# A mixer layer on one core: bank accesses in the planner's reckoning, one last block of 512 columns, and three column blocks at the start

## The chip, the cores and the metric

One of the eight cores of a Trainium2 chip runs the kernel. The metric is the device time of one execution in microseconds (us). A core has TensorE (PE, matrix products; PEld is its weight loading), VectorE (DVE), ScalarE (ACT), GpSimd (POOL) and SyncE (SP), each with an instruction stream of its own; they wait for one another by semaphores. SBUF is the on-chip memory that operands come from, PSUM the one that products are summed in, here eight banks of 128 x 512 numbers.

## The reference

One layer of a streaming encoder: 512 tokens of 2,048 numbers are projected, mixed along time by two groups of heads, projected back, added to the input and normalised.

```python
proj = einsum('btd,dc->btc', h, w_in)              # 2048 -> 8320 columns
rw = token_shift(proj[..., :RWKV_COLS], shift_mu)  # first 4224 columns
hg = proj[..., RWKV_COLS:]
o_rwkv = rwkv7_branch(rw, ...)   # 16 heads of 64: r, k, v, z and two low-rank parts
o_hgrn = hgrn2_branch(hg, ...)   # 8 heads of 128: q, f, i, z (g in the kernel)
y = einsum('btc,cd->btd', concatenate([o_rwkv, o_hgrn], -1), w_out)
h = layer_norm(ALPHA * h + y, ln_w, ln_b)
```

## The kernel before

Everything is in float32. A product of float32 accuracy is made of three of a faster kind: each operand is split into a rounded part (ScalarE copies it, suffix h) and the rest (VectorE subtracts, suffix l), and `three` multiplies h by h, h by l and l by h into one PSUM bank.

The tokens are transposed in 16 tiles of 128 channels x 512 tokens (`xh`, `xl`), which stay in SBUF. The projection goes by blocks of 128 columns (`proj`): 16 tiles x 3 products of 512 columns each. Weights come from `w_all` in loads of 512 KB into two raw buffers (`wr`); each holds two quarters, and a quarter is split into `wh` and `wl`, of which there are three each (`ready`, `part`). A raw buffer is loaded again when both its quarters are split.

At the start two column blocks, w0 (the low-rank columns) and k0, are multiplied together token tile by token tile while the tiles arrive. `first` fetches the weight quarters, `token` the tiles, all in SP's queue; the first weight quarter is cut after 128 columns. Nine products with a zero tile (`WARM`) run before.

Between the projection's products stand the mixers': per head pair a preparation, an inversion, a scan of eight chunks, and a finish for RWKV; per HGRN head masked products of chunks. Their small products write PSUM banks tagged `mix` (two) and `acc` (two), the projections the four `main` banks. The gated outputs of all heads (`gated`) are spilled and read again for the output projection.

What runs when is decided while the program is built, by `Plan`. It keeps an estimated clock for each engine and queues of threads (generators of operations). `until` and `three` advance TensorE's clock with the large products; `pump` issues the next operation of each thread whose operands are estimated to be ready at about the present time (`step`, `start`, `seen`). A product that a thread offers is issued only if its start, as `start` has it, is not later than TensorE's present time less a lead of 0.35 us; otherwise the next large products go first. The order of instructions on each engine is then fixed; on the chip each waits by semaphores for what it really needs, and that includes the last engine that used its PSUM bank.

The output projection goes by blocks of columns, and within a block by the 16 gated tiles (`rows`): each tile of weights is multiplied with four row blocks of 128 tokens, in four banks. There are three blocks of 512 columns and two of 256; of the last one, the row blocks are done one after another, from weights that are all split by then. For each row block and column block `row_out` adds the input (VectorE reads PSUM), takes statistics (`bn_stats`), and after the last column block `finish` computes mean and variance, GpSimd the power -1/2 of the variance (`rsqrt`), and then each row is normalised. In `finish` the first 512 to 768 columns (`POOL_COLS`) are scaled by ScalarE and multiplied and added to on GpSimd (`early`), the others are done on VectorE (`late`): times the norm's weight beforehand (`premultiply`), less the weighted mean, times the factor plus the norm's bias, two or three passes in all. Outputs leave from SP's queue and ScalarE's.

Of the kernel before, what the change touches and what calls it, by code (L numbers as in the profile page):

```python
# [15 lines left out]
P = 128  # L16
# [36 lines left out]

SETS = {AF.Sigmoid: ("sigmoid",), AF.Tanh: ("exp", "sigmoid"), AF.Exp: ("exp",)}


class Plan:
# [11 lines left out]
    def __init__(self, room):  # L69
        self.clock = {"pe": 0.0, "dve": 0.0, "act": 0.0, "pool": 0.0, "dma": 0.0}  # L70
        self.table = None
        self.narrow = False
        self.queues = []
        self.ready, self.busy = {}, {}
        self.room = room
        self.slots = {tag: [(0, 0.0)] * n for tag, n in room.items()}
        self.count, self.used = 0, {}

    def start(self, e, op):

        t = 0.0
        for r in op.reads:
            t = max(t, self.seen(r, e))
        for w in op.writes:
            x, by = self.busy.get(w, (0.0, e))
            if e != "pe" or by is None:
                t = max(t, x if by == e else x + self.AFTER[by])
        return t

# [117 lines left out]
def mixer_kernel(ctx, tc, x_t, x_r, w_all, par, up, ln_wb, consts, hmask, out):  # L207
# [25 lines left out]
    def take(tag, shape=(P, T), dt=F32):  # L233
# [5 lines left out]
        if tag in PBUFS:  # L239
            t = ppool.tile(list(shape), dt, tag=tag, name=nm(tag), bufs=PBUFS[tag])  # L240
        else:
# [137 lines left out]
    def ready(i, tags=("wh", "wl")):  # L379

        if i < 2 * nload and i not in parts:
            parts[i] = tuple(st(t, [P, QT], F32R) for t in tags)

            def run():
                yield from split(*parts[i], raws[i // 2][:, i % 2 * QT : i % 2 * QT + QT])
                if i % 2:
# [19 lines left out]
    def part(i, width):  # L406
# [3 lines left out]
        plan.until(lambda: by_now(lo))  # L410
# [27 lines left out]
    def rows(q, width, lh, ll, fin, order=range(KT), hook=None, tags=("main",), early=None):  # L438
# [3 lines left out]
        for j in range(KT // per):  # L442
# [3 lines left out]
            for t in range(4):  # L446
                if j == 0:
                    pss.append(main_ps(tags)[:, :width])
                if early:
                    for i in early[j][t - 1 : t]:  # L450
                        ready(q + i, ("t", "t") if i in IN_T else ("wh", "wl"))
                elif 0 < t < 3:
# [605 lines left out]
    u0, u1 = unit(), unit()  # L1058
# [5 lines left out]
    plan.clock["pe"] = T0  # L1064
# [3 lines left out]
    def first(q, tag):  # L1068

        if q >= 4:  # L1070
            raw = take("g")
        elif q % 2 == 0:
# [4 lines left out]
        src = w_all[q // 2, :, q % 2 * QT : q % 2 * QT + QT]  # L1077

        def bring(c0, c1):
            nc.sync.dma_start(raw[:, c0:c1], src[:, c0:c1])  # L1080
            plan.fetched(raw, 4 * (c1 - c0))

            def run():
                if q not in parts:
                    parts[q] = tuple(st(t, [P, QT], F32R) for t in ((tag, tag) if tag else ("wh", "wl")))
                hi, lo = parts[q]
                yield from split(hi[:, c0:c1], lo[:, c0:c1], raw[:, c0:c1])
                if c1 < QT:
                    return
                if q >= 4:  # L1090
                    drop(raw)
                elif q % 2:
                    load(2 * u1 + 2 + q // 2)

            return run

        return bring

    def token(k):
# [8 lines left out]
        return run  # L1108

    plan.clock["dma"] = 0.7  # L1110
    arrive = []

    def fetch(k):
        a = []
        if k % 4 == 0:
            w0, w1 = first(4 * u0 + k // 4, None), first(4 * u1 + k // 4, "q4")
        if k == 0:

            a = [w0(0, P), token(k), w1(0, P), w0(P, QT), w1(P, QT)]
        elif k % 4 == 0:  # L1120
            a = [w0(0, QT), token(k), w1(0, QT)]
        else:
            a = [token(k)]
        arrive.append(a)

    for k in range(12):
        fetch(k)
    ps0, ps1 = main_ps(), main_ps()
    queued = 0
    for k in range(KT):  # L1130
        while queued < min(k + 5, KT):
            for run in arrive[queued]:
                plan.add(splits, run())
            queued += 1
        if 2 <= k < 6:
            plan.until(room(t=1))
# [3 lines left out]
        if k >= 13:  # L1140
            ready(4 * u1 + k - 9)
        qs = (4 * u0 + k // 4, 4 * u1 + k // 4)
        plan.until(lambda: by_now(xl[k]) and all(q in parts and by_now(parts[q][1]) for q in qs))
        for ps, q in zip((ps0, ps1), qs):
            hi, lo = (a.rearrange("p (k c) -> p k c", c=P) for a in parts[q])
            three(ps, hi[:, k % 4], lo[:, k % 4], xh[k], xl[k], k == 0, k == KT - 1)
# [58 lines left out]
    for name, j in _order()[1:]:  # L1205
# [30 lines left out]
        if (name, j) == ("k", 0):  # L1236
            ps = ps1
# [10 lines left out]
    sums, earlies, norms = plan.queue(), plan.queue(), plan.queue()  # L1248
    stats = cpool.tile([P, 4, 5, 6], F32, tag="stats", name="stats")
# [3 lines left out]
    POOL_COLS = (768, 640, 512, 512)  # L1253
    blocks = [(0, 512), (512, 512), (1024, 512), (1536, 256), (1792, 256)]
# [6 lines left out]
    def cuts(c0, c1):  # L1261

        return [(max(c0, d * T), min(c1, d * T + T)) for d in range(4) if max(c0, d * T) < min(c1, d * T + T)]

# [3 lines left out]
    def premultiply(t, c0, c1):  # L1268

        c0 = max(c0, POOL_COLS[t])  # L1270
        if c0 < c1:
            y, w = ys[t][c0 // T][:, c0 % T : (c1 - 1) % T + 1], lnw[0][:, 0, c0:c1]
            k = y_keys(t, c0, c1)
            yield keyed(Op([dve_tt_way(y, y, w), pool_tt_way(y, y, w)], [], []), k, k)

    def finish(t):
        mv, rs = take("mv", [P, 4]), take("rs", [P, 1])
        k_st, k_mv, k_v, k_n, k_r, k_m = ([f"{n}{t}"] for n in ("stat", "mean", "var", "neg", "rstd", "bias"))
        yield keyed(Op([("dve", 0.1, lambda: dve.bn_aggr(mv[:, 0:2], stats[:, t]))], [], []), k_st, k_mv + k_v)
        yield keyed(ts(mv[:, 1:2], mv[:, 1:2], LN_EPS, None, ALU.add), k_v, k_v)  # L1280
        yield keyed(ts(mv[:, 2:3], mv[:, 0:1], -1.0, None, ALU.mult), k_mv, k_n)
# [185 lines left out]
```

## Time and profile before

| | us |
|---|---|
| median of three runs (lowest, highest) | 1121.27 (1120.59, 1122.06) |
| the profiled execution | 1123.09 |
| its span, first to last instruction | 1121.3 |
| TensorE busy in it | 1091.5 |
| VectorE, ScalarE, GpSimd busy | 766.5, 456.3, 88.6 |

A row of a profile gives start and length in us, the engine, the line, the operation with the tile written, an arrow and the tiles read, the size in partitions x elements, and in brackets how long the engine was idle before and what it waited for. "x3" stands for three instructions in a row. TensorE's products are pipelined: their starts follow one another every 0.23 us while each is shown 0.39 us long. The granted clock is the share of TensorE's full clock that the chip lets through; on average it was 0.991.

### The profile page before, as it was taken

Reading aid. Unit: us, or ns where it says so; the run is one execution under the profiler, and the core shown is the slowest. Engines: PE = TensorE matmul, PEld = TensorE weight load, DVE = VectorE, ACT = ScalarE, POOL = GpSimd, SP = SyncE. Lnnn points to the kernel's source line nnn. Section 1 sums busy time; section 2 is a strip of 40 time slices with the busy share of each in tenths; the row PEclk is TensorE's granted clock in tenths of the full one; section 3 lists DMA queues with packets and bytes.
Section 4 is the critical chain, followed back from the end, with each engine's and each line's share of the span. In section 5 each row is a group of like instructions: output and inputs, shape, how many; then the busy total and the mean of one; then the engine's idle time right before and its main releaser. Section 6 shows DMA issues by size and latency. Waiting matters only on the chain.

```text
span 1121.3 us, 19205 instructions
## 1 busy us (share of the span) xinstructions
PE 1091.5 (97%) x7402; PEld 901.8 (80%) x7402; DVE 766.5 (68%) x1739; ACT 456.3 (41%) x1042; POOL 88.6 (8%) x163
## 2 busy tenths in 40 slices
PE   8999999999999999999999999999999999999994
PEld 7878878788888878788887888888887778888893
DVE  6658967645579767857986774657976776624468
ACT  6532365433332465534245552433346444322221
POOL 0000000000010000101000010001000010000015
PEclk8999999999999999999999999999999999999997
DMA  7222211133323311223231122322231145433433
GB/s 274 85 80 93 95 59 58 57 99 94 90 75 103 96 58 59 67 79 117 76 104 58 58 76 87 99 92 77 94 102 46 52 141 194 136 122 110 144 126 138
DMA packets 36667, 108.50 MB, mean 97 GB/s; under 512 B 4320, under 2 KB 6496, under 8 KB 36448
## 3 DMA queue, kind: packets, MB, share of 16 engines
q1 hardware_dynamic: 34848, 104.33, 29.2%
q10 hardware_dynamic: 1728, 2.95, 0.7%
q8 instruction: 58, 0.95, 0.4%
q14 instruction: 33, 0.27, 0.1%
HBM read 99.92 MB, written 7.34 MB: 96 GB/s over the span
## 4 chain that ended last, share of the span: by engine, by line
PE 89%; DVE 6%; ACT 2%; issue 1%; DMA 1%; POOL 0%; SPq 0%; DVEq 0%; ACTq 0%
PE main L396 68%; PE mix L288 10%; PE mix L396 3%; PE acc L396 3%; PE acc L288 3%; PE mix L292 2%; DVE q L320 1%; DVE wl L311 1%; DVE t L311 1%; ACT z L301 1%; DVE bd L320 1%; ACT wh L301 1%; DMA t<-x_t 0%; DVE inv L320 0%; DMA t<-spill 0%
## 5 line engine op out<-in xcount | busy, mean ns | idle before, releaser
L396 PE MATMUL main<-xh,wh 128*128 128x512 f32 x896 | 358.0, 400 | 2.2 <-ACT xh L301 2.2
L396 PE MATMUL main<-xh,wl 128*128 128x512 f32 x896 | 356.6, 398 | 0.0
L396 PE MATMUL main<-xl,wh 128*128 128x512 f32 x896 | 356.0, 397 | 0.0
L301 ACT ACTIVATE wh<-wr 128x512 fp32r<-128x512 f32 (+1 forms) x313 | 195.5, 626 | 268.9 <-PE main L396 203.9
L311 DVE TENSOR_TENSOR wl<-wr,wh 128x512 fp32r<-128x512 f32 (+1 forms) x313 | 213.5, 683 | 130.2 <-ACT wh L301 126.9
L396 PEld LDWEIGHTS main<-xh,wh 128*128 128x128 f32 x896 | 169.1, 189 | 36.0 <-ACT xh L301 2.6
L396 PEld LDWEIGHTS main<-xl,wh 128*128 128x128 f32 x896 | 168.9, 188 | 33.8 <-DVE xl L311 0.8
L396 PEld LDWEIGHTS main<-xh,wl 128*128 128x128 f32 x896 | 168.9, 189 | 33.5
L396 PE MATMUL main<-wh,xh 128*128 128x512 f32 (+1 forms) x272 | 108.0, 397 | 1.9 <-DVE t L320 1.9
L396 PE MATMUL main<-wh,xl 128*128 128x512 f32 (+1 forms) x272 | 108.1, 397 | 0.0
L396 PE MATMUL main<-wl,xh 128*128 128x512 f32 (+1 forms) x272 | 107.4, 395 | 0.0
L301 ACT ACTIVATE z<-mix 64x64 f32<-64x64 f32 (+1 forms) x245 | 56.0, 229 | 92.1 <-DVE bd L320 71.4
L396 PEld LDWEIGHTS main<-wh,xh 128*128 128x128 f32 x272 | 51.3, 189 | 10.4 <-DVE t L320 2.3
L396 PEld LDWEIGHTS main<-wh,xl 128*128 128x128 f32 x272 | 51.3, 189 | 8.6
L396 PEld LDWEIGHTS main<-wl,xh 128*128 128x128 f32 x272 | 51.3, 189 | 8.2
L302 ACT ACTIVATE t<-main,om 128x512 f32<-128x512 f32 x33 | 22.6, 688 | 61.2 <-PE main L396 61.1
L320 DVE SCALAR_TENSOR_TENSOR bd<-mix,pc,bd 64x64 f32<-64x64 f32 x112 | 31.2, 283 | 22.4 <-PE mix L288 17.2
L343 POOL TENSOR_TENSOR rs<-rs,mhalf 128x8 f32<-128x8 f32 (+1 forms) x16 | 25.1, 1572 | 250.3 <-DVE rs L316 129.5
L311 DVE TENSOR_TENSOR inv<-inv 64x30 f32<-64x30 f32 (+14 forms) x120 | 38.6, 322 | 3.1
L311 DVE TENSOR_TENSOR inv<-inv,inv 64x30 f32<-64x30 f32 (+14 forms) x120 | 38.6, 322 | 2.9
L346 POOL MEMSET z<- 64x128 f32 x64 | 11.9, 199 | 355.7 <-PE acc L288 312.1
L311 DVE TENSOR_TENSOR t<-t,tot 128x256 f32<-128x256 f32 x96 | 38.4, 416 | 0.2
(207 smaller groups left out, 1489.1 us busy)
## 6 DMA issues: line engine op xcount, KB each, us to landing
wr<-w_all SPq DMA_DIRECT2D x158, 512.0 KB, 3.5
t<-x_t SPq DMA_DIRECT2D x16, 256.0 KB, 5.6
g<-x_r SPq DMA_DIRECT2D x16, 256.0 KB, 4.2
spill<-g SPq DMA_DIRECT2D x12, 256.0 KB, 4.3
t<-spill SPq DMA_DIRECT2D x12, 256.0 KB, 4.0
big<-ln_wb SPq DMA_DIRECT2D x1, 2048.0 KB, 9.1
out<-q ACTq DMA_DIRECT2D x7, 256.0 KB, 2.4
up<-up SPq DMA_DIRECT2D x8, 128.0 KB, 2.8
```

The lines of the kernel that those rows point to most:

```text
L288: return Op([("pe", cost, lambda: pe.matmul(o, l, r, start=start, stop=stop, **kw))], [l, r], [o], narrow=narrow)
L292: return Op([("pe", 0.11, lambda: pe.transpose(o, i, ident))], [i], [o])
L301: return "act", cost, lambda: sc_e.activation(o, i, f, scale=scale)
L302: return "act", cost, lambda: sc_e.activation(o, i, f, scale=scale, bias=bias)
L311: return dve_op([a, b], o, lambda: dve.tensor_tensor(o, a, b, f), base=0.16 if o.shape[0] < P and size(o) == C and o.tensor.name in tags e ...
L320: return dve_op([a, b], o, lambda: dve.scalar_tensor_tensor(o, a, s, b, f1, f2), per=0.00113, base=0.085 if o.shape[0] == P else 0.25 if s ...
L343: lambda: pool.tensor_tensor(o, i, mhalf[:, : size(o)], ALU.pow))], [i], [o])
L346: return Op([("pool", 0.1, lambda: pool.memset(o, v))], [], [o])
L396: pe.matmul(ps, l, r, start=first and i == 0, stop=last and i == 2)
```

## The change

There are three parts.

The planner. Each PSUM tile's name is kept in `banks`. An operation that reads a bank now counts as ready only after the bank's last use by any engine (`done`), and a product that writes one after the last use by another engine; before, a product that wrote a bank took no account of readers of the same tile.

The start. Three blocks, w0, k0 and r0, are multiplied together. The weight quarters of the first four tiles are cut in three, 128, 128 and 256 columns; the three first pieces are issued from ScalarE's queue, everything else from SP's. Tile 0's nine products go in the order h by h for the three blocks, then l by h, then h by l.

The end. The last 1,024 columns are two blocks of 512. The weights of the last one are fetched along with those of the one before, in alternation (`_last_quarters`), and are kept split in SBUF, in tiles tagged `t`, `ksq` and `ia` that the mixers no longer need and in `wh` and `wl`. Its row blocks follow one another, as those of the last 256 columns did. GpSimd computes only the rsqrt. Of each row block all four pieces of 512 columns are scaled by ScalarE and multiplied and added to by VectorE; in the last row block ScalarE and VectorE share them, the first two (`AHEAD`) going the way of `late`. All outputs leave from SP's queue.

```diff
@@ class Plan
         for r in op.reads:
             t = max(t, self.seen(r, e))
+            if r in self.banks:
+                t = max(t, self.done(r, e))
         for w in op.writes:
-            x, by = self.busy.get(w, (0.0, e))
-            if e != "pe" or by is None:
-                t = max(t, x if by == e else x + self.AFTER[by])
+            t = max(t, self.done(w, e))
         return t
+
+    def done(self, name, e):
+        x, by = self.busy.get(name, (0.0, e))
+        return (0.0 if e == "pe" else x) if by == e else x + self.AFTER[by]
@@ start
-    u0, u1 = unit(), unit()
+    us = [unit() for _ in range(3)]
...
+            ws = [first(a, 0) for a in range(3)]
+            for bring, run in ws:
+                bring(0, P, nc.scalar)
+            x0 = token(0)
+            for bring, run in ws:
+                bring(P, 2 * P)
...
+            fetch(1)
+            for bring, run in ws:
+                bring(2 * P, QT)
...
+        if k == 0:
+            for i, (low, x) in enumerate(((0, xh[0]), (1, xh[0]), (0, xl[0]))):
+                for ps, q in zip(pss, qs):
...
+                    begin_one(ps, parts[q][low][:, :P], x, i)
@@ end
+def _last_quarters():
+    o = [(2, 0)] + [(d, n + 3 - d) for n in range(13) for d in (2, 3)]
+    return o + [(2, 14), (2, 15), (3, 13), (3, 14), (3, 15)]
...
-    POOL_COLS = (768, 640, 512, 512)
-    blocks = [(0, 512), (512, 512), (1024, 512), (1536, 256), (1792, 256)]
...
+        def last(d):
+            y, w, b, o, k = columns(d)
+            if d in first:
+                yield keyed(stt(y, y, rs, b, ALU.mult, ALU.add), k + k_r, k)
+            else:
+                yield keyed(tt(y, y, b, ALU.add), k, k)
+            nc.sync.dma_start(o, y)
...
+        for d in rest:
+            y, w, b, o, k = columns(d)
+            yield keyed(Op([("act", 0.6, lambda y=y: sc_e.activation(
+                y, y, AF.Identity, scale=rs, bias=mv[:, 3:4]))], [], []), k + k_r + k_m, k)
```

At the start, SP's queue (x_t are token tiles, w_all the weights, into wr, g and t for the three blocks), before:

```order
L1080 DMA wr_122<-w_all 128x128
L1101 DMA t_125<-x_t 128x512
L1080 DMA g_123<-w_all 128x128
L1080 DMA wr_122<-w_all 128x384
L1080 DMA g_123<-w_all 128x384
L1101 DMA t_130<-x_t 128x512
```

and now:

```order
L1117 DMA t_128<-x_t 128x512
L1092 DMA wr_122<-w_all 128x128
L1092 DMA g_123<-w_all 128x128
L1092 DMA t_124<-w_all 128x128
L1117 DMA t_133<-x_t 128x512
L1092 DMA wr_122<-w_all 128x256
```

Token tile 0 is now SP's first transfer and tile 1 its fifth, where they were the second and the sixth; the three small pieces for tile 0 have gone to ScalarE's queue, whose beginning is now:

```order
L1092 DMA wr_122<-w_all 128x128
L1092 DMA g_123<-w_all 128x128
L1092 DMA t_124<-w_all 128x128
L313 ACT_TABLE_LOAD
L313 ACTIVATE wh_170<-wr_122 128x128
L313 ACTIVATE xh_68<-t_128 128x512
```

It began with the table load and the same two splits; the three issues stand ahead of them.

In the scans of the mixers' second group, on TensorE (rt, z, bt, bd are tiles of a scan, main<-xh products of the projection), before:

```order
L288 MATMUL acc_4212<-bd_3737,q_2928 128x128
L292 MATMUL mix_4230<-cst,q_2929 128x128
L396 MATMUL main_4123<-xl_90,wh_4086 128x512
L396 MATMUL main_4123<-xh_74,wl_4087 128x512
L288 MATMUL acc_4222<-bd_3718,q_2550 128x128
L292 MATMUL mix_4241<-cst,q_2551 128x128
L292 MATMUL mix_4241<-cst,t_2846 128x128
```

and now:

```order
L300 MATMUL acc_4319<-bd_3730,q_2562 128x128
L411 MATMUL main_4103<-xh_82,wh_4216 128x512
L411 MATMUL main_4103<-xl_98,wh_4216 128x512
L304 MATMUL mix_4378<-cst,q_2563 128x128
L304 MATMUL mix_4378<-cst,t_2858 128x128
L411 MATMUL main_4103<-xh_82,wl_4217 128x512
```

Between a scan's product into acc and the transposes into mix that follow it stand two products of the projection now, where they followed one another; the places differ all along the scans in this way.

At the end, VectorE's work on the last row block, from its evacuation on (g is the input, big the norm's weight and bias, inv the row block, mv and rs its statistics), before:

```order
L320 SCALAR_TENSOR_TENSOR inv_9737<-g_10561,main_10833 128x256
L1336 BN_STATS stats<-inv_9737 128x6
L1279 BN_AGGR mv_10910<-stats 128x2
L316 TENSOR_SCALAR mv_10910<-mv_10910 128x1 x2
L333 TENSOR_TENSOR inv_9737<-inv_9737,big_9548 128x256
L320 SCALAR_TENSOR_TENSOR inv_9736<-big_9548,mv_10910,inv_9736 128x512
L320 SCALAR_TENSOR_TENSOR inv_9737<-big_9548,mv_10910,inv_9737 128x512
L320 SCALAR_TENSOR_TENSOR inv_9736<-inv_9736,rs_10911,big_9548 128x512
L320 SCALAR_TENSOR_TENSOR inv_9737<-big_9548,mv_10910,inv_9737 128x512
L320 SCALAR_TENSOR_TENSOR inv_9737<-inv_9737,rs_10911,big_9548 128x512 x2
```

and now:

```order
L332 SCALAR_TENSOR_TENSOR inv_9749<-g_10645,mix_10623 128x512
L1389 BN_STATS stats<-inv_9749 128x6
L1331 BN_AGGR mv_10700<-stats 128x2
L328 TENSOR_SCALAR mv_10700<-mv_10700 128x1 x2
L332 SCALAR_TENSOR_TENSOR inv_9748<-big_9587,mv_10700,inv_9748 128x512
L332 SCALAR_TENSOR_TENSOR mv_10700<-mv_10700,rs_10701 128x1
L332 SCALAR_TENSOR_TENSOR inv_9748<-big_9587,mv_10700,inv_9748 128x512
L332 SCALAR_TENSOR_TENSOR inv_9748<-inv_9748,rs_10701,big_9587 128x512
L323 TENSOR_TENSOR inv_9749<-inv_9749,big_9587 128x512
L332 SCALAR_TENSOR_TENSOR inv_9748<-inv_9748,rs_10701,big_9587 128x512
L323 TENSOR_TENSOR inv_9749<-inv_9749,big_9587 128x512 x3
```

Evacuation and statistics are 512 wide instead of 256, the multiplication that stood behind them is gone, the bias of the row (mv from rs) has come over from GpSimd, and two pieces take a multiplication and an addition behind ScalarE's scaling.

More of the change, by code (lines that the diff above doesn't have):

```diff
@@ L1384, in mixer_kernel @@
     for t in range(4):
         sl = slice(t * P, t * P + P)
[L1386 removed]
+        ps = main_ps(banks)
         for n, k in enumerate(korder):
[L1388 to L1390 removed]
+            if t == 0 and n == 1:
+                quarters(len(seq))
+            if n == 4:
+                residual(t, 3)
+            hi, lo = part(q0 + seq.index((3, n)), T)
+            three(ps, gh[k][:, sl], gl[k][:, sl], hi, lo, n == 0, n == KT - 1)
```

313 lines of the change are left out of this document (175 added, 138 removed).

## Prediction

> **What bounds the kernel now.** I read the page first, then busy time by stretch, then the timeline of the first 17 us and the last 65 us, then who waited for whom. The page says TensorE:
>
> ```profile
> span 1121.3 us, 19205 instructions
> PE 1091.5 (97%) x7402; PEld 901.8 (80%) x7402; DVE 766.5 (68%) x1739; ACT 456.3 (41%) x1042; POOL 88.6 (8%) x163
> ```
>
> TensorE is idle for 29.8 us of the span. Nothing the change does removes a product, so its gain has to come out of those 29.8 us, out of stretches where TensorE is busy at a worse rate, or out of the work after its last matmul. The next rows (columns: stretch, its length, then busy time of PE, PEld, DVE, ACT, POOL, the granted clock, DMA share, GB/s) say where the idle time in the middle lies.
>
> ```profile
> 25.00:900.00 875.00, 867.43 (x6182) 709.34 (x6180) 620.44 (x1471) 375.96 (x901) 56.85 (x127) 1.00 0.26 81
> 900.00:950.00 50.00, 47.71 (x276) 39.03 (x275) 37.77 (x87) 22.96 (x49) 5.85 (x3) 1.00 0.45 152
> 950.00:1104.00 154.00, 154.00 (x869) 135.54 (x868) 80.66 (x137) 38.68 (x64) 15.56 (x15) 1.00 0.41 136
> ```
>
> 875 us hold 7.57 us of idle TensorE, the 50 us after them 2.29, the last 154 none. So three places matter: the start, the mixers (9.86 us in all), and the end.
>
> **Part 1, the start.**
>
> ```profile
> 0.74 0.38 SPq L1080 DMA_DIRECT2D wr<-w_all  x1
> 3.06 1.38 SPq L1101 DMA_DIRECT2D t<-x_t  x3
> 4.92 0.64 PE L396 MATMUL main<-xh,wh 128*128 128x512 f32 x1
> 6.55 0.39 PE L396 MATMUL main<-xh,q 128*128 128x512 f32 x1
> 8.40 2.01 ACT L301 ACTIVATE xh<-t 128x512 fp32r<-128x512 f32 x3 [0.33 <-DMA t<-x_t]
> 9.09 0.80 PE L396 MATMUL main<-xh,wh 128*128 128x512 f32 x1 [2.15 <-ACT xh L301]
> 8.50:9.00 0.50, 0.00 (x0) 0.00 (x0) 0.16 (x1) 0.50 (x1) 0.00 (x0) 0.68 1.06 410
> 9.09 30.21 PE main L396 x118
> 1014.94 43.52 PE main L396 x192
> ```
>
> The last row is the rate of undisturbed 512-wide products: 43.52 / 192 = 0.2267 us each. TensorE does the six products of token tile 0 from 4.92 to 6.55 and then sits 2.15 us until tile 1, issued at 3.06, has landed at 8.4 and been split. In that gap the granted clock falls: 0.68 in the half microsecond 8.5 to 9.0 means that it fell to half at about 8.7. The chain row has 118 products take 30.21 us from 9.09; at 0.2267 they need 26.75, so the half clock costs 3.46. The start loses 9.09 - 6 x 0.2267 + 3.46 = 11.2 us against a TensorE that were busy from time 0.
>
> With three column blocks tile 0 feeds nine products and tile 1 nine more. Tile 1 is then the transfer that completes 896 KB of arrivals (six weight pieces of 64 KB and two tiles of 256 KB) where it completes 1,024 KB now (64 + 256 + 64 + 192 + 192 + 256), and it is the fifth issue on SP instead of the sixth: at SP's spacing of 0.47 us (0.74 to 3.06 is five issues) it goes out at 2.6. The first three pieces leave from ScalarE's queue, ahead of its table load, so splitting begins later, at about 3.4 instead of 2.7, but tile 0 is what the first product waits for and it leaves 0.43 earlier. Bounds for the start of tile 1's products: 9.09 as now (twice as many small pieces may eat what is saved) and 7.0, where the nine products of tile 0, from about 4.9, end and nothing is waited for. I take 8.3, in the upper half: 0.44 for the issue, and of one eighth of the 5.3 us between its issue and its landing (0.67) half, since small pieces moved slowly. With the nine products done at 7.0 TensorE waits 1.3 us, not 2.15. From there it has 9 x 0.2267 = 2.04 us of work per token tile, more than ScalarE's 2.01 / 3 = 0.67 per tile plus three weight splits every four tiles, so it should not wait again beyond some 0.3 us for the second half of the first weight quarters. If the clock stays whole the start then loses 8.3 - 9 x 0.2267 + 0.3 = 6.6: a gain of 4.6. If it falls again, 3.46 of this is lost: a gain of about 1.2.
>
> Does it fall? The gap of 2.15 us did it. A gap of the same kind later did not:
>
> ```profile
> 920.68 0.50 PE L396 MATMUL main<-wh,xh 128*128 128x512 f32 x1 [1.92 <-DVE t L320]
> ```
>
> Here TensorE was idle 1.92 us and the row of 900 to 950 above keeps a granted clock of 1.00. So 1.3 us should be survived; I give that 0.7. The Trainium skill, "TensorE: Matmul & The Clock Gate", section on the HAM clock gate, says that the clock is halved only after an idle window of about 3.4 us. By that rule neither gap would have halved it, and no gap of 1.3 us would; the row at 8.5 disagrees, so the rule does not raise the chance above what the two rows give.
>
> The other work of the third block is only moved: its 48 products, 4 weight splits on ScalarE and VectorE and 1 MB of loads stood in the first block's successors before. SP gets no wait that was not there; ScalarE's queue holds three issues ahead of its first split.
>
> **Part 2, the last 512 columns and the norm.** Now two blocks of 256 columns:
>
> ```profile
> 1058.46:1081.49 23.03, 23.03 (x194) 23.03 (x194) 14.67 (x26) 8.19 (x14) 1.17 (x1) 1.00 0.55 183
> 1081.49:1104.53 23.04, 23.04 (x193) 22.83 (x191) 21.01 (x43) 2.73 (x4) 11.98 (x13) 1.00 0.24 89
> ```
>
> 384 products of 256 columns take 46.07 us, with weight loading busy all the time; 192 of 512 take 43.52. That is 2.55 us off TensorE with nothing beside it, so off the end.
>
> After TensorE's last matmul (end 1104.53) VectorE is still at work on the third row block:
>
> ```profile
> 1109.81 0.41 DVE L320 SCALAR_TENSOR_TENSOR inv<-g,main 128x256 f32<-128x256 f32 x1
> 1110.71 0.29 DVE L1279 BATCH_NORM_AGGREGATE mv<-stats 128x2 f32<-128x30 f32 x1
> 1111.04 0.21 DVE L316 TENSOR_SCALAR mv<-mv 128x1 f32<-128x1 f32 x2
> 1111.27 0.72 POOL L343 TENSOR_TENSOR rs<-mv,mhalf 128x1 f32<-128x1 f32 x1 [1.93 <-DVE mv L316]
> 1111.50 1.41 DVE L320 SCALAR_TENSOR_TENSOR inv<-big,mv,inv 128x512 f32<-128x512 f32 x2
> 1112.33 0.81 ACT L1294 ACTIVATE inv<-inv,mv,rs 128x512 f32<-128x512 f32 x1 [6.21 <-DMA out<-q]
> 1113.49 1.75 DVE L320 SCALAR_TENSOR_TENSOR inv<-big,mv,inv 128x512 f32<-128x512 f32 x1
> 1115.16 2.41 DVE L320 SCALAR_TENSOR_TENSOR inv<-inv,rs,big 128x512 f32<-128x512 f32 x2
> 1056.03 0.39 PE L396 MATMUL main<-wh,xl 128*128 128x512 f32 x1
> 1056.46 0.69 DVE L320 SCALAR_TENSOR_TENSOR q<-g,main 128x512 f32<-128x512 f32 x1 [2.04 <-PE main L396]
> 1057.18 0.69 DVE L1336 BATCH_NORM_STATS2 stats<-q 128x6 f32<-128x512 f32 x1
> 1068.81 1.29 DVE L311 TENSOR_TENSOR t<-wr,t 128x512 fp32r<-128x512 f32 x2
> ```
>
> The last block's evacuation starts at 1109.81, 5.28 us after TensorE ended. From there the chain is 11.49 us to the end of the span, of which the last 3.73 (1117.57 to 1121.3) are the output's transfer. Next to GpSimd's two 512-wide operations a VectorE operation of 0.74 took 1.75.
>
> In the new block each row block has 48 x 0.2267 = 10.88 us on TensorE. VectorE's chain for one of the first three, by these rows: evacuation 0.72, statistics 0.72, aggregate 0.33, variance 0.13, GpSimd's rsqrt to 1.05 after that, bias and ScalarE's first scaling 1.05 (0.81 and two hand-overs), eight multiplications or additions at 0.61 (1.29 for two) 4.9: 8.9 us. It is done 2 us before the next block arrives, so the backlog of 5.28 goes, and the last evacuation starts 0.43 after the start of the last product (1056.03 to 1056.46). Its own chain from the evacuation on: 0.72 + 0.72 + 0.33 + 0.13, first mean subtraction 0.66 beside the rsqrt, bias at 2.85, second subtraction to 3.6, then two scale-and-add at 0.66 and four multiplications or additions at 0.61, the last to its full 0.69: 7.42. ScalarE's two scalings (2 x 0.81 from 3.05, so to 4.6) are finished before VectorE asks for them at 4.26 and 5.5. With 3.73 for the output 11.15 us, against 11.49: wider evacuation and statistics cost 0.6, GpSimd's absence gives more than that back.
>
> So, in the time of this execution: last product at 1058.30 + 191 x 0.2267 = 1101.6, evacuation at 1102.0, end at 1113.2: 8.1 us earlier, 2.5 of it TensorE's and 5.6 the tail's.
>
> Against it stand the loads. The weights of the last two blocks now all come interleaved, two quarters for each 2.72 us of products (12 x 0.2267) over 13 steps, through two raw buffers.
>
> ```profile
> 1068.14 1.15 ACT L301 ACTIVATE t<-wr 128x512 fp32r<-128x512 f32 x2 [0.38 <-DMA wr<-w_all]
> 1068.91 0.33 SPq L376 DMA_DIRECT2D wr<-w_all  x1
> 1074.92 0.33 SPq L376 DMA_DIRECT2D wr<-w_all  x1
> DMA to landing us min/median/max: 3.4/3.7/5.4
> ```
>
> One buffer's round was 6.0 us there (1068.91 to 1074.92); 3.7 to landing and 2.0 for the two splits (1068.14 to 1070.1) make 5.7. The two buffers must come round every 5.44. Each round loses 0.3 to 0.6, over six and a half rounds 2 to 4 us, against a lead of two steps less the split, about 2.7 at its start. I charge 0.5 us; bounds 0 and 3.4 (6.5 x 0.56, and 0.65 for each of four residual tiles that join the queue, less the lead). End part: 7.6.
>
> **Part 3, the mixers.** The planner now lets an operation on a PSUM bank wait for the bank's last user, as the chip does.
>
> ```profile
> PE acc L288 <- DVE t L311: 2.4, 8, 0.4
> PE mix L288 <- DVE nr L327: 1.7, 2, 0.8
> ```
>
> Such waits, of a small product behind VectorE, are what the 9.86 us of idle consist of. Where the planner expects them, it puts projection products in front: in the order of the program, from the first to the last acc-from-bd product of a group's scans, there are 135, 136, 144 and 147 of them before and 157, 159, 171 and 176 after, with the number of changes between large and small products all but equal (638 and 642). The products themselves are only moved, and TensorE is full beside them, so I cost the moving at nothing; if the scans got longer in time, the cover is the projection, which after the last small product still has 677 products (641 before) to run. Bounds: the whole 9.86 gained, or 3 lost (the 1.92 wait above and one of 0.8 once more). I take 4, less than half: one wait of 1.92 is for the evacuation of a projection, which the rule does not touch, and late operands remain late.
>
> **Sum.** 4.6 + 7.6 + 4.0 = 16.2. The profiled execution took 1123.09 us with a span of 1121.3, so 1106.9 with a span of 1105.1. The median of the runs is 1121.27, 1.8 below that execution: 1105.1.
>
> **Rivals.** (1) The clock falls at the start all the same: 1105.1 + 3.4 = 1108.5. For it: it did, and the gap may be longer than 1.3. (2) The planner's rule moves products and frees nothing, since the late operands are late for other reasons: 1109.1; for it, the 1.92 wait. (3) The last blocks' weights come late as bounded above: 1105.1 + 2.9 = 1108.0; against it, TensorE has no idle time in 950 to 1104 with buffers at the same round. (4) Slower: the scans' chain stretches in time. It has 56 acc-from-bd steps, two heads side by side, so 28 in a row; 16.2 us of gain are gone if each is later by 0.58 us and the output blocks then wait for the last gated tiles. But 36 more products (8.2 us) stand between, so it decides from 24.4 / 28 = 0.87 us a step, and gives 1121.3 + 28 - 24.4 = 1124.9 at 1 us a step. The planner's 22 to 29 more products per group are 5 to 6.6 us for 7 steps, of this size; against it, the small products end earlier in the order, not later.
>
> **Chances.** Forecast 0.42, (1) 0.25, (2) 0.16, (3) 0.1, (4) 0.03; 0.04 for all of the mixers' idle time gained (1099). Two of the middle rivals together give 1112. Range 1100 to 1113. 0.2% is 2.2 us, about what the measurement tells from no change: faster 0.95, same 0.02, slower 0.03.
>
> **What will show it.** Start: first product of token tile 1 near 8.3 and no stretch at clock 0.5. End: from the last product's start to the end of span 11.6 us, VectorE idle before the last evacuation, no VectorE operation above 0.8. Loads: no idle TensorE in the last 170 us. Mixers: idle time of 25 to 950 near 6. The prediction is wrong if tile 1 lands no earlier, or if the mixers' idle time grows.

## The result, and the profile after

| | before | after |
|---|---|---|
| median of four runs each, us (lowest, highest) | 1120.93 (1120.41, 1122.06) | 1092.95 (1092.63, 1093.53) |
| the profiled execution, us | 1123.09 | 1093.0 |
| its span, us | 1121.3 | 1091.2 |

The ratio is 0.975 (95% interval 0.9733 to 0.9767): 28.0 us faster in the medians, 30.1 in the two profiled executions. The forecast was 1105.1 with a range down to 1100; the time lies below the range. The page of after, its span and engines:

```profile
span 1091.2 us, 18722 instructions
PE 1078.4 (99%) x7210; PEld 892.3 (82%) x7210; DVE 767.8 (70%) x1785; ACT 451.1 (41%) x1001; POOL 66.3 (6%) x145
```

Busy time by stretch, after (stretch, length, then PE, PEld, DVE, ACT, POOL, clock, DMA share, GB/s):

```profile
25.00:900.00 875.00, 874.89 (x6293) 724.21 (x6292) 648.03 (x1578) 377.96 (x876) 57.01 (x128) 1.00 0.28 84
900.00:950.00 50.00, 50.00 (x251) 42.09 (x251) 33.75 (x59) 20.99 (x39) 5.07 (x4) 1.00 0.49 173
950.00:1079.90 129.90, 129.90 (x574) 107.27 (x572) 64.97 (x108) 35.77 (x58) 1.64 (x3) 1.00 0.45 138
```

The 9.86 us of idle TensorE between 25 and 950 are down to 0.11. More telling is the third number: in the same 875 us TensorE was shown loading weights for 709.34 us before and for 724.21 after. More of the program passed through the same time, by 2.1%, although the busy time of the products grew by only 0.9%.

The start of after, in the timeline:

```profile
4.47 0.33 SPq L1092 DMA_DIRECT2D wr<-w_all  x1
7.73 0.39 PE L411 MATMUL main<-xh,wh 128*128 128x512 f32 x1
9.77 1.32 ACT L313 ACTIVATE xh<-t 128x512 fp32r<-128x512 f32 x2 [0.58 <-DMA t<-x_t]
10.45 0.50 PE L411 MATMUL main<-xh,wh 128*128 128x512 f32 x1 [0.43 <-ACT xh L313]
11.18 0.50 PE L411 MATMUL main<-xl,wh 128*128 128x512 f32 x1 [0.23 <-DVE xl L323]
```

Token tile 1's first product is at 7.73 instead of 9.09 and waits for nothing; tile 2's wait instead. Against full rate (the start of the 61st large product less 60 x 0.2267) the start loses 7.2 us where it lost 11.0: 3.8 gained between these two executions.

The end of after:

```profile
1079.90 0.40 PE L411 MATMUL mix<-wh,xl 128*128 128x512 f32 x1
1080.33 0.69 DVE L332 SCALAR_TENSOR_TENSOR inv<-g,mix 128x512 f32<-128x512 f32 x1 [2.37 <-PE mix L411]
1082.31 0.55 POOL L355 TENSOR_TENSOR rs<-mv,mhalf 128x1 f32<-128x1 f32 x1 [10.43 <-DVE mv L328]
1083.19 1.52 ACT L1372 ACTIVATE inv<-inv,mv,rs 128x512 f32<-128x512 f32 x2 [8.14 <-DVE mv L332]
1084.50 3.40 SPq L1353 DMA_DIRECT2D out<-inv  x4
1085.66 1.89 DVE L323 TENSOR_TENSOR inv<-inv,big 128x512 f32<-128x512 f32 x3
```

VectorE has nothing left to do 2.37 us before the last evacuation, and from the last product's start to the end of the span it is 11.3 us (1079.90 to 1091.2), where it was 17.05 (1104.25 to 1121.3). With the 2.55 us of the merged block the end gives 8.3. The account is then 30.1 - 3.8 - 8.3 = 18.0 us for the mixers, of which 9.75 were idle time that the profile showed. Where were the other 8? The timeline of before has places like this one (start, length):

```profile
409.17 0.40 PE L396 MATMUL main<-xl,wh 128*128 128x512 f32 x1
409.41 0.39 PE L396 MATMUL main<-xh,wl 128*128 128x512 f32 x1
409.93 0.49 PE L288 MATMUL mix<-z,bt 128*128 128x128 f32 x2
```

The first two rows start 0.24 us apart, at about the undisturbed rate. The third starts 0.52 us after the second: TensorE stood still for some 0.29 us. But the second is shown 0.39 us long, so only 0.13 us of it looks idle, too little for a bracket. Where a wait is shorter than about 0.16 us (0.39 - 0.227) nothing of it shows. One can add up what the starts say: for every single product between 25 and 1,050 us the time to the next start, less the median of that time for products of its shape. Before this comes to 42.8 us, after to 25.2. Of the 17.7 between them 10.0 are at the step from a large product to a small one (22.4 and 12.4), 4.9 between small products and 2.6 between large ones. The sum is a rough measure: with other ways of sorting the products into kinds the difference comes out between 13 and 24 us, while that of the step from large to small stays near 10.

The Trainium skill says in "Perfetto Trace Analysis", section "Identifying the Most-Contended Engine", that the busy share of matmuls is not a good measure of how close TensorE is to its limit, because they are pipelined, and that the busy share of weight loading is one of two to use instead. The rows above agree: 97% and 99% busy hide what 709.34 and 724.21 us of loading show.

### The profile page after: what moved, and what is told of

It is laid out like the page before. It is cut to its first block, busy times and chain, and to the rows that moved or that the text cites. A ratio compares the mean times of both kernels' runs of the same rounds, so it can differ in the third digit from the quotient of the medians.

```text
span 1091.2 us, 18722 instructions
## 1 busy us (share of the span) xinstructions
PE 1078.4 (99%) x7210; PEld 892.3 (82%) x7210; DVE 767.8 (70%) x1785; ACT 451.1 (41%) x1001; POOL 66.3 (6%) x145
## 4 chain that ended last, share of the span: by engine, by line
PE 96%; DMA 2%; DVE 1%; SPq 0%; issue 0%; ACT 0%; DVEq 0%; ACTq 0%
PE main L411 72%; PE mix L300 11%; PE mix L411 4%; PE acc L411 4%; PE mix L304 2%; PE acc L300 2%; DMA pr<-par 1%; DMA t<-x_t 1%; DMA wr<-w_all 1%; DMA g<-w_all 0%; DVE inv L332 0%; DVE inv L323 0%; SPq L1092 0%; DVE xl L323 0%; SPq L1117 0%
## 5 line engine op out<-in xcount | busy, mean ns | idle before, releaser
L411 PE MATMUL main<-xl,wh 128*128 128x512 f32 x879 | 350.2, 398 | 0.3 <-DVE xl L323 0.2
L411 PE MATMUL main<-xh,wh 128*128 128x512 f32 x879 | 349.5, 398 | 0.4 <-ACT xh L313 0.4
L411 PE MATMUL main<-xh,wl 128*128 128x512 f32 x879 | 349.6, 398 | 0.0
L323 DVE TENSOR_TENSOR wl<-wr,wh 128x512 fp32r<-128x512 f32 (+1 forms) x305 | 207.4, 681 | 87.9 <-ACT wh L313 84.8
L411 PE MATMUL main<-wh,xl 128*128 128x512 f32 x256 | 103.4, 404 | 0.0
L411 PE MATMUL main<-wh,xh 128*128 128x512 f32 x256 | 103.1, 403 | 0.0
L411 PE MATMUL main<-wl,xh 128*128 128x512 f32 x256 | 103.0, 403 | 0.0
L313 ACT ACTIVATE z<-mix 64x64 f32<-64x64 f32 (+1 forms) x180 | 42.2, 235 | 67.6 <-PE mix L304 32.2
L365 DVE COPY z<-mix 64x64 f32<-64x64 f32 (+1 forms) x140 | 31.6, 226 | 14.8 <-PE mix L300 12.8
L332 DVE SCALAR_TENSOR_TENSOR t<-main,pr,t 128x511 f32<-128x511 f32 x33 | 24.5, 747 | 20.6 <-ACT t L314 20.2
```

The costliest lines, as they stand in the source:

```text
L313: return "act", cost, lambda: sc_e.activation(o, i, f, scale=scale)
L323: return dve_op([a, b], o, lambda: dve.tensor_tensor(o, a, b, f), base=0.16 if o.shape[0] < P and size(o) == C and o.tensor.name in tags e ...
L332: return dve_op([a, b], o, lambda: dve.scalar_tensor_tensor(o, a, s, b, f1, f2), per=0.00113, base=0.085 if o.shape[0] == P else 0.25 if s ...
L365: f = lambda: dve.tensor_copy(o, i)
L411: pe.matmul(ps, l, r, start=first and i == 0, stop=last and i == 2)
```

## Experiments

The times below are medians; each group ran beside the kernel before, whose median was 1121.34 (the first four), 1120.40 (the next four) and 1121.23 (the last four).

**The parts alone.** The kernel before with the planner's part alone:

```diff
             t = max(t, self.seen(r, e))
+            if r in self.banks:
+                t = max(t, self.done(r, e))
         for w in op.writes:
-            x, by = self.busy.get(w, (0.0, e))
-            if e != "pe" or by is None:
-                t = max(t, x if by == e else x + self.AFTER[by])
+            t = max(t, self.done(w, e))
```

> The kernel before with the planner's part alone (start and end as before). Theory A, hidden waits: the idle time that the profile of before shows for TensorE in 25 to 950 us (9.86 us) is only part of what it waits there, since a product shown 0.39 us long covers a wait of up to 0.16 us behind it. The span fell by 30.1 us; 4.0 of it can be read at the start (time lost against full rate 11.0 and 7.0 us) and 8.3 at the end (2.55 for the products, 5.75 from the last product's start to the end, 17.05 and 11.3); 17.8 are left, and all of them come from the planner. So this kernel takes about 1121 - 17.8 = 1103 us, and the sum of all pitches above the median of their kind falls from 42 us to about 24. Rival B, visible idle only: the planner gives at most the 9.86 us that show, so 1111 us, and the other 8 us come from the third block at the start or from the new end.

With the start alone (the diff of `first`, `fetch` and the loop over token tiles):

> The kernel before with the new start alone (three blocks together), planner's reckoning and end as before. Theory A: only the start's own 4.0 us are gained, so 1117 us, the first product of token tile 1 at about 7.7 us and no fall of the granted clock. Rival B: the missing 8 us come from here, because the first group of heads gets its r block earlier: 1109 us, and the idle time of TensorE in 25 to 950 us is clearly below 9.9.

With the end alone (`_last_quarters`, `finish`, the last blocks):

> The kernel before with the new end alone (last block of 512 columns, norm on VectorE and ScalarE), planner's reckoning and start as before. Theory A: 2.55 us for the products and 5.75 for the tail, 8.3 in all, so 1112.7 us; from the last product's start to the end of the span 11.3 us. Rival B: the missing 8 us lie here: 1104.5.

And the changed kernel with the planner's old reckoning:

> The changed kernel with the planner's old reckoning (new start, new end). Theory A: 4.0 + 8.3 = 12.3 us below before, so 1108.7 us, 15.7 above the changed kernel. Rival B (8 us of start or end): about 1100.5. A third possibility, that the parts help each other, shows as a difference between this kernel's gain and the sum of the gains of the start alone and the end alone.

| kernel | us | against before, 95% interval of the ratio |
|---|---|---|
| planner alone | 1103.32 | -18.0 (0.9826 to 0.9859) |
| start alone | 1117.87 | -3.5 (0.9958 to 0.9980) |
| end alone | 1112.82 | -8.5 (0.9912 to 0.9942) |
| start and end, old reckoning | 1109.41 | -11.9 (0.9885 to 0.9915) |

Theory A (hidden waits) gave 1103, 1117, 1112.7 and 1108.7; rival B is off by 8 to 9 us in each. (The expectations count 4.0 us for the start where the account above has 3.8.) The parts add up: 3.5 and 8.5 make 12.0, measured 11.9. Busy time by stretch of the planner alone:

```profile
25.00:900.00 875.00, 875.00 (x6291) 724.77 (x6290) 645.65 (x1567) 376.24 (x870) 55.41 (x127) 1.00 0.27 84
```

No idle time is left, and weight loading is as dense as in after. 875 x (1 - 709.34 / 724.77) = 18.6 us: so much sooner is the work of before's 875 us done at this density, against 18.0 measured. The sum over the starts is 24.7 us, 18.1 less than before's 42.8.

**What in the rule does it.** In the kernel before, the half of the rule that is about writing changes nothing in the order of any engine's instructions; the half about reading alone gives, on TensorE, the order of the whole rule through all the mixers. What it concerns are banks that ScalarE and VectorE both read: the second reader waits for the first. In the scans, ScalarE copies the next chunk's z out of the bank from which VectorE updates bd. ScalarE's waits for it between 25 and 950 us, before (total, times, longest):

```profile
ACT z L301 <- DVE bd L320: 71.4, 44, 3.1
```

and after:

```profile
ACT z L313 <- DVE bd L332: 12.7, 12, 1.6
```

The planner that knows of the wait gives both reads to one engine more often: 119 `mix` banks of the program have readers on both engines before, 56 after. So two explanations stood against each other, fewer hand-overs (A) and better places on TensorE (B), and a third, that any more cautious reckoning would do (C); from here on the letters stand for these. First, z always on VectorE, planner as before (`dve_copy` is `copy` with VectorE as its only engine):

```diff
                 for h in range(2):
-                    yield copy(zs[(c + 1) % 3][0:64, hc[h]], block(pd, h, P))
+                    yield dve_copy(zs[(c + 1) % 3][0:64, hc[h]], block(pd, h, P))
```

> The kernel before, planner as before, but in the scans the copies of the next chunk's z out of the bank that bd is updated from go to VectorE always (before, the planner chose ScalarE or VectorE). Theory A, shared banks: what the rule frees are hand-overs between two readers of one bank. In the trace of before ScalarE waits 71.4 us in 44 places for VectorE's bd before it copies z out of the same bank, after the change 12.7 in 12; z is what the next chunk's products wait for. With both readers on VectorE this hand-over is gone although the planner reckons as before: 1121 less 8 to 18 us, I say 1109. Theory B, the order on TensorE: only a planner that knows the waits puts projection products in front of the small ones, so without the rule the gain is under 3 us: above 1118.

The rule used for the choice of the engine alone, and the opposite (`start` uses the rule where `shared` is true; the first of the two values is for the choice of the engine, the second for the times, and in the opposite kernel they change places):

```diff
-            r = self.start(e, op)
...
+            for shared in (True, False):
+                r = self.start(e, op, shared)
+                s = max(r, self.clock[e]) + turn
+                ends.append(s + cost)
+            c.append((ends[0], ends[1], s, r, e, f))
-        return min(c, key=lambda x: x[0])
+        return min(c, key=lambda x: x[0])[1:]
```

> The kernel before, with the new rule used only where the planner chooses the engine of an operation; when an operation is taken as ready is reckoned as before. Theory A, shared banks: engine choice is what counts (in the program, the mix banks read by both ScalarE and VectorE fall from 119 to 47, with the whole rule to 55): 12 or more of the 18 us, below 1109. Theory B: the times count, so under 6 us are gained: above 1115.

> The opposite half: the engine is chosen by the old rule, readiness is reckoned by the new one (83 mix banks are read by both engines). Theory A: the hand-overs largely stay and the chain of a scan stays long, but TensorE gets projection products in front: under 9 us, above 1112. Theory B: most of the 18 us: below 1109.

And the old rule with twice the lead:

```diff
-    LEAD = -0.35
+    LEAD = -0.7
```

> The kernel before with the lead doubled, from 0.35 to 0.7 us: a product is offered only when its operands are reckoned ready 0.7 us ago, with the old rule (107 mix banks read by both engines). Rival C, any caution does it: a reckoning that is too early by a hand-over is mended by any later one: 10 us or more gained, below 1111. Theories A and B: the error lies in single operations, up to 3 us each, and a lead that is the same for all costs the scans time: less than 6 us gained, 1115 to 1124.

Each of the four gained most of it: 1106.17 (-14.2; ratio 0.9856 to 0.9889), 1104.53 (-15.9; 0.9841 to 0.9870), 1102.52 (-17.9; 0.9820 to 0.9852) and 1104.94 (-15.5; 0.9845 to 0.9875). One of the four runs of the third took 3799.46 us, for a reason that no trace shows; the other three lie between 1101.77 and 1102.70, with a median of 1102.33. The rows of 25 to 900 us, z on VectorE:

```profile
25.00:900.00 875.00, 873.83 (x6239) 721.70 (x6240) 655.01 (x1601) 363.56 (x813) 58.96 (x128) 1.00 0.27 84
```

engine choice alone:

```profile
25.00:900.00 875.00, 873.82 (x6273) 723.43 (x6274) 641.89 (x1553) 378.07 (x876) 57.41 (x128) 1.00 0.27 84
```

times alone:

```profile
25.00:900.00 875.00, 874.92 (x6292) 724.37 (x6292) 637.03 (x1528) 385.18 (x916) 56.69 (x128) 1.00 0.27 84
```

and the lead of 0.7:

```profile
25.00:900.00 875.00, 874.48 (x6282) 721.36 (x6283) 630.22 (x1501) 387.43 (x928) 54.71 (x127) 1.00 0.27 84
```

By the density of weight loading these should be worth 15.0, 17.0, 18.2 and 14.6 us. My A and B both fall as single causes, since either half suffices, and C, which I held for the unlikely one, is right about the size. With the lead of 0.7 half of the hand-overs' waits are still there (ScalarE waits 36.9 us in 34 places for bd), and 107 `mix` banks are still read by both engines. What the four have in common is on TensorE, which takes its instructions in order. Counted as in the prediction, the scans of the four groups hold 562 products of the projection before, 658 in the planner alone, and 629, 605, 627 and 658 in these four; and the time lost at the step from a large to a small product falls from 22.4 us to 14.1, 11.1, 11.7 and 14.9 (11.8 in the planner alone). So TensorE comes less often to a small product whose operand is not there yet.

**One cause or two.** The changed kernel without the rule, but with the lead of 0.7:

> The changed kernel with the planner's old reckoning and the lead of 0.7 us. On the kernel before the doubled lead alone gained 15.5 us, the rule 18.0. Theory D, one cause: all of these mends take away the same waits of TensorE, those of small products that are issued ahead of their operands, and what is left of them is close to none in each; so this kernel comes to 1109.4 (new start and end, old reckoning) less 15.5, 1094, within 2 us of the changed kernel's 1093. Rival E: the rule gives something that caution does not (fewer hand-overs, a shorter chain of scans), which counts once the end follows sooner: 1097 or more.

It took 1093.35 us (ratio 0.9740 to 0.9769), 0.4 above the changed kernel, which is less than the intervals can tell: theory D. The rule gives nothing here, as far as these runs can show, that plain caution does not give. Both together, the rule and the lead of 0.7, were not run. And the opposite, the changed kernel with all its rules and no lead (`LEAD = 0.0`):

> The changed kernel, rule and all, with the lead set to 0: a product is offered as soon as its operands are reckoned ready at TensorE's time. Theory D: the waits of TensorE come back although the rule stands, since an operand that is late by a few tenths of a us holds up all the products behind: 5 to 20 us slower than 1093, with the time between products grown by more than the idle time that shows. Rival E (shared banks are what cost): within 3 us of 1093.

1096.21 us (0.9763 to 0.9795), 3.3 slower: between the two expectations, and so a miss for both. Its rows:

```profile
25.00:900.00 875.00, 874.76 (x6273) 720.15 (x6271) 647.50 (x1569) 379.89 (x881) 55.96 (x129) 1.00 0.28 84
900.00:950.00 50.00, 49.14 (x258) 40.68 (x257) 29.28 (x55) 20.45 (x39) 4.97 (x3) 1.00 0.50 174
```

Waits do come back, as D says: the sum over the starts is 28.5 us instead of 25.2, while in the first stretch hardly more idle time shows than in after (0.24 and 0.11 us). But with the reckoning right, 0.35 us less lead costs a fifth of what 0.35 us more lead gained with the reckoning wrong. The number of products in front does not decide alone: the scans of this kernel hold 536, fewer than before's.

**The start's new wait.** In the program each transfer waits for the landing of the one issued eight before it. In after the ninth, SP's first piece of 256 columns, waits until 4.47 for the first, a 64 KB piece that left ScalarE's queue at 0.73; SP issues nothing from 3.01 on. With two pieces for three:

```diff
             for bring, run in ws:
-                bring(0, P, nc.scalar)
+                bring(0, 2 * P, nc.scalar)
             x0 = token(0)
-            for bring, run in ws:
-                bring(P, 2 * P)
```

> The changed kernel with the first weight quarters cut in two, 256 and 256 columns, instead of three pieces. Each transfer in the program waits for the landing of the one issued eight before it; the ninth, SP's first 256-column piece, waits in the profile of the changed kernel until 4.47 us for the first, which left at 0.73 and lands late, so SP issues nothing for 1.46 us. With two pieces the first eight hold both token tiles and all three quarters, and token tile 2 is the ninth instead of the twelfth. If that stall feeds TensorE's waits at 10.0 to 11.4 us (0.43 and 0.23 us, with slow products between them; the start loses 7.0 us), 0.5 to 1.2 us are gained: about 1092.2. Rival: the larger pieces delay token tile 0 and the first product by as much, and nothing changes: 1093.0, first product later than 5.6 us.

And, against that kernel, with the first block's first piece from SP's queue:

```diff
-            for bring, run in ws:
-                bring(0, 2 * P, nc.scalar)
+            for (bring, run), by in zip(ws, (nc.sync, nc.scalar, nc.scalar)):
+                bring(0, 2 * P, by)
```

> As the kernel with pieces of 256 columns, and the first block's first piece leaves from SP's queue ahead of token tile 0 instead of ScalarE's. In the profile of before such a piece (64 KB) issued by SP at 0.74 was split at 2.70, in that of the changed kernel one issued by ScalarE at 0.73 was split at 4.48, just ahead of token tile 0. If its split is done early, the first product waits for the tile's split alone, 0.2 to 0.3 us sooner: 1092.0. Rival: the tile, issued 0.4 us later, lands as much later, and the time is that of the other kernel or up to 0.4 us more.

The first took 1093.60 us (0.9742 to 0.9771). In its timeline the first product starts at 6.25 and SP's ninth transfer, now token tile 2, leaves even later:

```profile
5.36 0.33 SPq L1117 DMA_DIRECT2D t<-x_t  x1
```

The stall is not gone, since the larger piece from ScalarE's queue lands later still, at about 5.36. The start loses 8.0 us, but not all of this is the stall's:

```profile
8.35 0.63 PE L1163 MATMUL main<-xh,q 128*128 128x512 f32 x1
8.78 0.63 PE L1163 MATMUL main<-xh,inv 128*128 128x512 f32 x1
9.20 0.50 PE L1163 MATMUL main<-xl,wh 128*128 128x512 f32 x1
```

These products start 0.43 us apart, as those of before did between 10.40 and 11.26 under a granted clock of 0.50; in after they start 0.23 apart from 5.92 on. (The windows show 1.00 there, but the records of the clock begin in this trace only at 9.43.) The four steps from 7.92 to 9.54 take 1.62 us where four at full rate take 0.91. About 0.7 of the 8.0 us is thus a slow start of this execution and not the stall. The rival of the expectation (1093.0, first product later than 5.6) was the nearer.

The second removes the stall: its ninth transfer leaves at 3.5, and no idle time shows between its products from token tile 1 on:

```profile
5.75 0.50 PE L1163 MATMUL main<-xh,wh 128*128 128x512 f32 x1 [0.71 <-ACT xh L313]
7.94 0.39 PE L411 MATMUL main<-xh,wh 128*128 128x512 f32 x1
10.23 0.39 PE L411 MATMUL main<-xh,wh 128*128 128x512 f32 x1
```

Its start loses 6.15 us, 1.1 less than after's, and the profiled execution took 1091.35. But its other runs took 1092.18, 1094.13 and 1094.23, and the median, 1093.16 (0.9736 to 0.9765), is not below the changed kernel's. The first product, forecast 0.2 to 0.3 us sooner, came at 5.75 instead of 5.36, as the rival had it. Why the time spreads over 2.9 us is open. First products at half the rate, as in the execution just shown, could make up a part of it, but no trace of the slower runs was kept. A kernel that beats the changed one has not been shown.

## Why the prediction was wrong, point by point

**The mixers, sized 4.0 us, measured 18.0: the step that failed.** The prediction said that "nothing the change does removes a product, so its gain has to come out of those 29.8 us" of idle time, "out of stretches where TensorE is busy at a worse rate", or out of the end. It then bounded the mixers by the first alone, "the whole 9.86 gained", and took less than half. The second source was named and not looked at. It could have been: the starts of before's timeline gave 42.8 us over the usual pitch, and 22.4 of them at the step from a large to a small product. That is not the gain itself, since 25.2 are left in after, but it is far above 9.86. Within the bound the choice of 4.0 was wrong too: "late operands remain late" does not matter when other products stand in front. Even the wait of 1.92 us that "the rule does not touch" is gone: with the planner alone TensorE is busy for the whole of 900 to 950 us. The places on TensorE and on VectorE had all moved; which of them did it is not shown. That the rule concerns two readers of one bank, and that the half about writing does nothing, I did not see.

**The start, 4.6 us, measured 3.8 between the profiles and 3.5 in the medians.** Tile 1 came at 7.73, not 8.3, and the clock did not fall. But I counted on 0.3 us of further waiting and there were 1.5 (7.2 less 7.73 - 9 x 0.2267), at tile 2, behind the chain of eight transfers; without that stall, in the trace of the last experiment, no product of tile 2 shows a wait. The two errors partly cancel: the change's start loses 7.2 us where I had 6.6. The prediction put 3.46 of its 4.6 on the half clock. In the four traces with before's start in which the clock stayed whole (the last section), the start loses 8.6 to 9.2 us up to the 91st large product, where before loses 11.0 and after 7.2. So the half clock is about 2 of the 3.8 us, and before does not pay it in every execution.

**The end, 7.6 us, measured 8.5 alone, 8.3 in the trace.** The mechanism held: 11.3 us from the last product (predicted 11.6), VectorE idle 2.37 us before the last evacuation (predicted 2), no VectorE operation of one row above 0.75 in the tail (predicted 0.8). The 0.5 us charged for late weights was not needed: the stretch from 950 to the last product's start has no idle time.

**The rivals.** Rival 1 did not occur: the granted clock did not fall at the start, here or in any of the six other traces with the new start. But the argument for it, that a gap of 1.3 us is survived, was not put to the test, since TensorE had no such gap before tile 1; and the last section shows that the length of a gap did not decide. Rival 3 (late weights) did not occur either. Rival 2 (the planner frees nothing) and rival 4 (the scans get longer until the output waits) were both refuted by the planner alone. The forecast's 0.04 for "all of the mixers' idle time gained" (1099) is what came closest, and it still lacked 8 us of the mixers' gain and 6 us of the time. The three terms as measured alone, 18.0, 3.5 and 8.5, make 30.0 against 28.0 for the whole; the intervals of these ratios are some 3 us wide, so the difference is not resolved.

## What to carry to other kernels

Idle time is a lower bound of what an in-order, pipelined engine waits: where its instructions are shown longer than their pitch, compare starts with the usual pitch, or the density of weight loading, before you bound a gain by what looks idle. When an engine's order is fixed while the program is built, an instruction issued a little too early can hold up all the others: here that cost some 15 to 18 us, while the later issue cost nothing that shows, since other work was there to fill in. Try the plain remedy, more lead, before a better reckoning. A cut of a transfer into more pieces takes places in whatever limits the transfers under way, and the piece that lands last there sets when the next may leave.

## What the hardware showed that was not expected

In three of the profiled executions with before's start the clock was halved for about 3.4 us or for twice that. In the planner alone, whose TensorE was idle for 1.72 us before token tile 1, the windows of the clock (the number after POOL's) show it:

```profile
10.00:10.50 0.50, 0.38 (x2) 0.34 (x3) 0.49 (x2) 0.48 (x2) 0.00 (x0) 1.00 1.09 418
10.50:11.00 0.50, 0.50 (x3) 0.42 (x2) 0.50 (x2) 0.49 (x2) 0.00 (x0) 0.64 1.05 406
14.00:14.50 0.50, 0.50 (x3) 0.40 (x3) 0.50 (x2) 0.44 (x2) 0.00 (x0) 0.95 1.04 389
```

0.64 in the second row means half speed from about 10.64, 0.95 in the third whole speed from about 14.05: 3.4 us. In the profiled execution of before it was from 8.68 to 15.51, 6.8 us. The two starts are the same instructions, and they lose 10.3 and 11.0 us; with the end alone, where the gap was 1.73 us, the half clock lasted 3.4 us and the start lost 9.5. In the four other kernels with the same instructions at the start (z on VectorE, engine choice alone, times alone, lead of 0.7) gaps of 1.98, 1.86, 2.21 and 1.60 us left the clock whole, and the starts lost 8.2, 8.0, 8.4 and 7.6, counted in the same way. The longest of them:

```profile
9.09 0.49 PE L406 MATMUL main<-xh,wh 128*128 128x512 f32 x1 [2.21 <-ACT xh L311]
6.00:16.00 10.00, 7.56 (x32) 5.66 (x31) 7.81 (x13) 7.69 (x13) 0.00 (x0) 1.00 1.01 354
```

So a gap of 1.72 us was followed by a fall and one of 2.21 was not: the length of the gap does not decide, and the prediction's comparison of 2.15 with 1.92 said nothing. The spread of before's runs over 2.6 us (in the first group 1120.24 to 1122.82, at mean clocks of 0.994 and 0.991) fits this, though those runs have no trace; so does the profiled execution of before, which was longer than any of them and made the start look a little more expensive than it is in the median. The Trainium skill, "TensorE: Matmul & The Clock Gate", part on the HAM clock gate, speaks of a free-running window of activity of about 3.4 us; the lengths of 3.4 and 6.8 agree. No gap here was that long, so a wholly idle window is not needed for the fall. That it depends on where the gap lies in such a window would fit the seven traces, but none of them shows it.
